# First rows of x sent ahead of the constants; odd layer's output weights further ahead in the order, no mix row in their staging buffers

## The chip, the cores and the metric

The kernel runs on one core of a Trainium2 chip. The metric is device time in microseconds (us), median of three runs; the kernel before takes 2293.11 us (2287.74 to 2295.61). Besides these there is one profiled execution, from which all rows below are taken.

## The reference, cut to what matters

Two layers over a sequence of 2048 rows of 1024 float32 values, each x <- x + RMSNorm(mixer(RMSNorm(x))). The even layer's mixer runs retention and stick-breaking attention side by side; the odd layer's runs a gated linear recurrence (HGRN2) and an RG-LRU. Both end the same way: the parts, each gated, are concatenated to eight blocks of 128 columns ("mix") and multiplied by an output matrix.

```python
def odd_mixer(h, w_in, w_out, lb, ...):
    proj = jnp.einsum('bsd,de->bse', h, w_in)
    hq, hf, hi, hg, lx, lg = split_cols(proj, ODD_SIZES)
    hc = rms_norm(hgrn2(hq, hf, hi, lb)).reshape(B, S, HG_VW) * jax.nn.silu(hg)
    hl = rg_lru(causal_conv(lx, ...), ...) * jax.nn.silu(lg)
    mix = jnp.concatenate([hc, hl], axis=-1)
    return jnp.einsum('bse,ed->bsd', mix, w_out)
...
for layer in range(DEPTH):
    h = rms_norm(x, pre_norm_w[layer])
    ...
    x = x + rms_norm(y, post_norm_w[layer])
```

## The kernel before, in words

The sequence is worked in two halves of 1024 rows, so there are four stages: even layer half 0, half 1, odd layer half 0, half 1. Each has a mixer phase (`stick` or `hgrn`) and then an output phase (`out_phase`). Products are float32 made of three fp32r products: each operand is split into a high part (cast on ACT) and a low part (difference on DVE), and each product of 128 contraction rows is three matmuls.

**Weights.** `load_w` (L118 to 133) loads 512 KB into a staging tile `raw` (pool `wr`, two buffers, one DMA on SP's queue, L127), casts it to `wh` on ACT (L131) and subtracts to `wl` on DVE (L132). The input projections (`proj`, L152) and the output weights go through the same two `raw` buffers, which are handed out in the order of the program.

**Mix.** A finished mix block of 128 columns by 512 rows is stored to DRAM (`mix_store`, L209, tensors `mixd`), except for the last of the eight, which is put straight into the operands `mh`, `ml` (`mix_direct`, L218 and L219). In the output phase `mix_rows` (L221 to 229) loads the other seven blocks for 128 rows back (L225, tile `mr`), casts on ACT (L227) and subtracts on DVE (L228). `mh`, `ml` lie in the tiles that held the transposed input `xh`, `xl` of the same 512 rows, so they can be written only once the last projection of these rows has run.

**Output phase.** Its output weights for the first 512 columns come as four pieces of 256 contraction rows (`W[0]`, L589, into pool `w2`); then `mix_rows` for rows 0 to 7 of 128 (pool `o2`, two buffers); then for each of the eight row groups 24 matmuls (L633) into one PSUM bank, named in turn `pp`, `z`, `o`. With `EARLY[layer]` = 1, row group 0 is fetched before that, from inside the last gate projection of the mixer phase, and staged in one of the two `raw` buffers (in `lru`, `lg_proj`, L762 to 764). `EARLY` is 0 for the even layer and 1 for the odd one.

**Order.** The program is written as one sequence; a scheduler gives each engine, and SP's DMA queue, its own fixed order, and each engine then works strictly in that order. `tc.high_priority(offset=n)` makes the scheduler treat the instructions inside as if they stood n instructions earlier. `tc.issue_after(d)` puts a DMA behind another on the queue. Pools are opened and closed like a stack: the pools of `out_phase` (`w2` 4 x (4 + 4) KB a partition, `o2` 2 x 3.5 KB, ...) begin at the place where those of `hgrn` began (`lru1` with `bd`, `lx`, `xc`, `r`, `ig` of 4 KB each; `lru5` with four tiles `ht` of 4 KB; `lrug` with `gt` of 2 KB; then `hg1`, `hg`, `hg4`). The last readers of these are in the last gate projection: `gt` times `ht` on DVE (L770), then `mix_direct` of `gt` (L218, L219).

**Start.** SP's queue begins with the identity matrix (L51) and two loads of `pre_norm_w` (L54), then the rows of x (L94). Each row of 128 is squared on ACT (L97), scaled on DVE (L99), transposed on PE (L112) and split (L114, L115). `stick` also builds a constant `past` in PSUM, with a copy on ACT (L378).

Of the kernel before, what the change touches and what calls it, by code (L numbers as in the profile page):

```python
# [21 lines left out]
KD = D // 128  # L22
EPS = 1e-6
LAG = 2
SHIFT = 1
EARLY = (0, 1)
LEVELS = (2, 4, 8, 16, 32, 64)


# [1 line left out]
def tile_trunk(ctx: ExitStack, tc: tile.TileContext, a: dict, out: bass.AP):  # L31
    nc = tc.nc
# [15 lines left out]
        return (o_bank[-1] if tag == "o" else ps_p).tile([128, 512], F32, tag=tag, name=tag)  # L48

    ident = const.tile([128, 128], F32, name="ident")  # L50
    nc.sync.dma_start(out=ident, in_=a["c_ident"])  # L51
    pre_w = const.tile([128, 2, KD], F32, name="pre_w")
    for i in range(2):
        nc.sync.dma_start(out=pre_w[:, i, :], in_=a["pre_norm_w"][i].rearrange("(k p) -> p k", p=128))  # L54
    mhalf = const.tile([128, 4], F32, name="mhalf")
    nc.vector.memset(mhalf, -0.5)
    state = const.tile([128, 512], F32, name="state")
# [16 lines left out]
    def scope(es, name, bufs, **kw):  # L74
        return es.enter_context(tc.tile_pool(name=name, bufs=bufs, reuse_waits="tile", **kw))

    def scope_o(es, bufs):
        o_bank.append(scope(es, "po", bufs, space=PSUM))
        es.callback(o_bank.pop)
        return o_bank[-1]  # L80
# [6 lines left out]
    def prep_rows(es, layer, half, ahead=2):  # L87
        p2, p8 = scope(es, "pr2", ahead), scope(es, "pr8", 8)
        rows = []

        def row(tt):
            i = half * 8 + tt
            xr = p2.tile([128, D], F32, tag="xr", name="xr")
            nc.sync.dma_start(out=xr, in_=x_in[i * 128:(i + 1) * 128, :] if layer == 0 else x1d[i])  # L94
            xn = p8.tile([128, D], F32, tag="xn", name="xn")
            ss = sm_p.tile([128, 1], F32, tag="ss", name="ss")
            nc.scalar.activation(out=xn, in_=xr, func=AF.Square, accum_out=ss)  # L97
            r = rstd_of(ss, 1, D)
            nc.vector.tensor_scalar(out=xn, in0=xr, scalar1=r, scalar2=None, op0=ALU.mult)  # L99
            rows.append(xn)  # L100
        return rows, row, p2

    def prep_cols(rows, layer):
        xh, xl = [], []

        def step(g, k):
            if k == 0:
                xh.append(xt_p.tile([128, KD, 512], F32R, tag="xh", name="xh"))
                xl.append(xt_p.tile([128, KD, 512], F32R, tag="xl", name="xl"))
            ps = bank("tr")  # L110
            for j in range(4):
                nc.tensor.transpose(ps[:, j * 128:(j + 1) * 128], rows[g * 4 + j][:, k * 128:(k + 1) * 128], ident)  # L112
            wk, hv = pre_w[:, layer, k:k + 1], xh[g][:, k, :]
            nc.scalar.activation(out=hv, in_=ps, func=AF.Copy, scale=wk)  # L114
            nc.vector.scalar_tensor_tensor(out=xl[g][:, k, :], in0=ps, scalar=wk, in1=hv.bitcast(F32), op0=ALU.mult, op1=ALU.subtract)  # L115
        return (xh, xl), step
# [20 lines left out]
    def proj_w(layer, col):  # L137
        ready[layer, col] = load_w(w_in[layer][:, col:col + 128], KD, 128)
# [82 lines left out]
    def mix_rows(half, M, tt, pool, tag):  # L221
        g, o = tt // 4, (tt % 4) * 128
        mh, ml = mix_slot(M, g)
        mr = pool.tile([128, 1024 if tag == "raw" else 896], F32, tag=tag, name="mr")[:, 0:896].rearrange("p (k t) -> p k t", k=7)
        d = nc.sync.dma_start(out=mr, in_=mixd[half][g][:, :, o:o + 128])  # L225
        hv = mh[:, 0:7, o:o + 128]
        nc.scalar.copy(out=hv, in_=mr)  # L227
        nc.vector.tensor_tensor(out=ml[:, 0:7, o:o + 128], in0=mr, in1=hv.bitcast(F32), op=ALU.subtract)  # L228
        return d.ins
# [57 lines left out]
    def ret_gate(half, heads, xT, t_p, g_p, M):  # L287
        for h in heads:
            def use(g, ps):
                if h == 3 and g == 1:  # L290
                    for tt in range(EARLY[0]):
                        mix_rows(half, M, tt, wr_p, "raw")
# [76 lines left out]
    def stick(half, xT, M):  # L369
        with ExitStack() as es:  # L370
            kv_p, qr_p, q_p, a_p, b_p, wt_p, g_p, t_p, r_p = (scope(es, n, b) for n, b in (
                ("skv", 8), ("sqr", 2), ("sq", 2), ("sa", 6), ("sb", 9), ("swt", 3), ("sg", 3), ("stmp", 2), ("srt", 1)))
            past = scope_o(es, 1).tile([128, 512], F32, tag="past", name="past")
            build = t_p.tile([128, 512], F32, tag="sg", name="build")
            nc.vector.memset(build, 0.0)
            nc.gpsimd.affine_select(out=build[:, 384:512], in_=build[:, 384:512], compare_op=ALU.is_gt, fill=1.0,
                                    base=0, pattern=[[-1, 128]], channel_multiplier=1)
            nc.scalar.copy(out=past, in_=build)  # L378
            D_ = [({}, {}, {}, {}) for _ in range(4)]

            def pair_proj(pr):
# [67 lines left out]
            def att(pr):  # L449
# [76 lines left out]
                for u in units + [None] * (2 if pr == 3 else 0):  # L526
                    bt = []
                    for i in range(4):
# [4 lines left out]
                        if u is not None and i == 3:  # L533
                            todo.extend((clock[0] + 1 + SHIFT + sj, back, gather, u, bt, sj) for sj in range(4))
                        if todo and todo[0][0] <= clock[0]:
                            _, fn, then, v, b, sj = todo.pop(0)
                            pend.append((then, v, sj) + fn(v, b, sj))
                            yield 437
                        if len(pend) > LAG:
                            then, *args = pend.pop(0)  # L540
# [29 lines left out]
    def out_phase(layer, half, M, following):  # L570
        prep_row = prep_step = xT = None
        with ExitStack() as es:
# [5 lines left out]
            else:  # L578
                x_p = scope(es, "ox", 8)
            early = EARLY[layer]  # L580
            mrs = [None] * early
# [3 lines left out]
            def piece(c, q, pool):  # L585
                return load_w(w_out[layer][:, c * 512:(c + 1) * 512], 2, 512, pool, order[2 * q:2 * q + 2])

            with tc.high_priority(offset=300):
                W = [[piece(0, q, w2_p) for q in range(4)], []]  # L589
            with tc.high_priority(offset=300):  # L590
                for tt in range(early, 8):
# [119 lines left out]
    def lru(half, xT, p1, p5, gt_p, sg_p, M):  # L711
# [50 lines left out]
        def lg_proj(j):  # L762
            def use_g(g, ps):
                if j == 3 and g == 1:
                    for tt in range(EARLY[1]):
                        mix_rows(half, M, tt, wr_p, "raw")
# [164 lines left out]
    with ExitStack() as es:  # L931
        rows, row, _ = prep_rows(es, 0, 0, 8)
        xT, step = prep_cols(rows, 0)
        for tt in range(8):
            row(tt)
            if tt in (3, 5):
                proj_w(0, 2048 if tt == 3 else 2560)
            if tt % 4 == 3:
                for k in range(KD):
                    step(tt // 4, k)  # L940
    for n, (layer, half) in enumerate(steps):
        M = {}
        if layer == 0:
            stick(half, xT, M)
            if half == 1:
                nc.vector.memset(state, 0.0)
                odd_const()
        else:
            with ExitStack() as es:
                hgrn(es, half, xT, M)  # L950
        xT = out_phase(layer, half, M, steps[n + 1] if n + 1 < len(steps) else None)
# [52 lines left out]
```

## Time and profile before

| | us |
|---|---|
| median of 3 runs | 2293.11 |
| lowest, highest | 2287.74, 2295.61 |
| the profiled execution, its own time | 2291.19 |
| its span, first to last instruction | 2289.3 |
| TensorE busy in it | 2210.1 |

A row of the timeline gives start, duration, engine, line, operation, output <- input, and the count merged into the row; in brackets the idle time of the engine before it and what ended that. A row of the windows gives for each stretch the busy time of each engine with the number of its instructions, the granted TensorE clock (1.00 is 2.4 GHz, 0.50 is 1.2 GHz), the share of DMA engines busy and GB/s.

### The profile page before, as it was taken

What the parts mean: (1) busy time and instruction counts of PE and PEld (TensorE: products, weight loads), DVE (VectorE), ACT (ScalarE), POOL (GpSimd) and SP (SyncE); (2) the same over time, 40 slices, a digit from 0 to 9 for tenths busy, and PEclk for the clock granted to TensorE, in tenths of its full rate; (3) what the DMA queues carried; (4) which work ended last, traced back from release to release, by engine and by line L of the source; (5) the groups of instructions that cost most, each with busy time, mean ns of one, the idle gap of its engine ahead of it and who ended that gap; (6) DMA issues with size and microseconds to landing.
All of it is one profiled execution on the core that took longest, in us unless ns stands there. A gap on an engine that the chain in (4) does not pass through costs nothing.

```text
span 2289.3 us, 31577 instructions
## 1 busy us (share of the span) xinstructions
PE 2210.1 (97%) x11392; PEld 1800.8 (79%) x11392; DVE 1391.7 (61%) x2049; ACT 1092.3 (48%) x2178; POOL 696.3 (30%) x988
## 2 busy tenths in 40 slices
PE   7999999999999999999899999999999999999998
PEld 6888787777878888787777887778877877878777
DVE  5554666674577776878888554555555535455543
ACT  5443545553466666767676433243245323433331
POOL 0422234411055454555663001222230013122400
PEclk9999999999999999999999999999999999999999
DMA  6433334346432232322313641111116511111161
GB/s 192 109 111 104 111 107 116 94 151 202 153 84 79 69 91 60 93 66 76 93 54 110 219 148 37 42 38 39 49 51 213 187 47 33 42 37 42 58 214 74
DMA packets 235804, 222.89 MB, mean 97 GB/s; under 512 B 21248, under 2 KB 181376, under 8 KB 235648
## 3 DMA queue, kind: packets, MB, share of 16 engines
q1 hardware_dynamic: 235488, 220.35, 31.2%
q8 instruction: 90, 1.47, 0.3%
q14 instruction: 66, 0.54, 0.1%
q0 software_dynamic: 160, 0.52, 0.1%
HBM read 147.43 MB, written 52.43 MB: 87 GB/s over the span
## 4 chain that ended last, share of the span: by engine, by line
PE 78%; DVE 9%; ACT 4%; DMA 3%; issue 3%; POOL 2%; SPq 0%; DVEq 0%; POOLq 0%; ACTq 0%
PE pp L152 42%; PE pp L633 5%; PE o L633 4%; PE o L514 4%; PE tr L499 4%; PE z L633 4%; DVE a L486 2%; PE z L473 2%; PE z L472 2%; PE z L887 2%; PE tr L112 1%; PE z L740 1%; DVE wtl L504 1%; DVE xc L734 1%; DVE wl L132 1%
## 5 line engine op out<-in xcount | busy, mean ns | idle before, releaser
L152 PE MATMUL pp<-xh,wh 128*128 128x512 f32 x1664 | 688.2, 414 | 6.9 <-DVE rst L356 6.2
L152 PE MATMUL pp<-xh,wl 128*128 128x512 f32 x1664 | 657.1, 395 | 0.0
L152 PE MATMUL pp<-xl,wh 128*128 128x512 f32 x1664 | 655.3, 394 | 0.0
L489 POOL TENSOR_TENSOR b<-b,a 128x511 f32<-128x511 f32 (+2 forms) x320 | 315.6, 987 | 181.9 <-DVE a L486 108.0
L152 PEld LDWEIGHTS pp<-xh,wl 128*128 128x128 f32 x1664 | 312.8, 188 | 68.2 <-issue 1.4
L152 PEld LDWEIGHTS pp<-xh,wh 128*128 128x128 f32 x1664 | 313.9, 189 | 60.4 <-issue 3.0
L152 PEld LDWEIGHTS pp<-xl,wh 128*128 128x128 f32 x1664 | 314.5, 189 | 48.6 <-issue 0.5
L486 DVE TENSOR_TENSOR_SCAN a<-a,past 128x512 f32<-128x512 f32 x192 | 244.4, 1275 | 74.7 <-ACT a L476 73.9
L476 ACT ACTIVATE a<-z 128x512 f32<-128x512 f32 (+2 forms) x320 | 172.2, 538 | 234.6 <-PE z L473 193.2
L132 DVE TENSOR_TENSOR wl<-raw,wh 128x1024 fp32r<-128x1024 f32 x136 | 170.2, 1257 | 129.8 <-ACT wh L131 129.5
L131 ACT CAST wh<-raw 128x1024 fp32r<-128x1024 f32 x136 | 142.8, 1053 | 187.9 <-PE pp L152 164.0
L71 POOL TENSOR_TENSOR rs<-rs,mhalf 128x1 f32<-128x1 f32 (+1 forms) x96 | 67.0, 698 | 515.6 <-DVE rs L70 502.8
L504 DVE TENSOR_TENSOR wtl<-tr,wth 128x512 fp32r<-128x512 f32 (+1 forms) x320 | 190.4, 596 | 44.4 <-ACT wth L503 43.4
L503 ACT CAST wth<-tr 128x512 fp32r<-128x512 f32 (+1 forms) x320 | 169.8, 531 | 69.4 <-PE tr L499 67.8
L499 PE MATMUL tr<-ident,b 128*128 128x128 f32 x1088 | 175.1, 275 | 10.6 <-DVE wtl L504 9.8
L499 PEld LDWEIGHTS tr<-ident,b 128*128 128x128 f32 x1088 | 133.1, 140 | 58.3 <-DVE wtl L504 17.1
L477 ACT ACTIVATE b<-z 128x512 f32<-128x512 f32 (+2 forms) x320 | 171.1, 535 | 0.1
L481 DVE TENSOR_TENSOR_SCAN a<-a,past 128x128 f32<-128x128 f32 (+3 forms) x128 | 104.5, 817 | 90.2 <-ACT a L476 89.3
L514 PE MATMUL o<-wth,v 128*128 128x512 f32 (+1 forms) x320 | 126.2, 394 | 1.1 <-ACT mol L520 1.1
L859 POOL TENSOR_TENSOR kg<-kg,t 128x256 f32<-128x256 f32 x96 | 71.3, 743 | 173.0 <-PE z L887 107.6
L479 POOL TENSOR_SCALAR_AFFINE_SELECT b<-b 128x128 f32<-128x128 f32 x128 | 42.3, 330 | 262.7 <-ACT b L477 246.7
L472 PE MATMUL z<-k,qh 128*128 128x512 f32 (+2 forms) x320 | 119.1, 372 | 1.9 <-DMA qh<-qrh 1.6
(216 smaller groups left out, 3592.5 us busy)
## 6 DMA issues: line engine op xcount, KB each, us to landing
raw<-in_even_w_in SPq DMA_DIRECT2D x56, 512.0 KB, 3.8
raw<-in_odd_w_in SPq DMA_DIRECT2D x48, 512.0 KB, 3.8
xr<-in_x SPq DMA_DIRECT2D x32, 512.0 KB, 4.3
xr<-x1d SPq DMA_DIRECT2D x32, 512.0 KB, 4.3
mr<-mixd SPq DMA_DIRECT2D x32, 448.0 KB, 4.8
qh<-qrh SPq DMA_DIRECT2D x64, 128.0 KB, 2.3
ql<-qrl SPq DMA_DIRECT2D x64, 128.0 KB, 2.4
x1d<-y SPq DMA_DIRECT2D x16, 512.0 KB, 2.9
```

The source lines that it names most:

```text
L132: nc.vector.tensor_tensor(out=wl, in0=raw, in1=wh.bitcast(F32), op=ALU.subtract)
L152: nc.tensor.matmul(ps, w[:, k, :], xx[g][:, k, :], start=(n == 0), stop=(n == 3 * KD - 1))
L472: nc.tensor.matmul(z[:, 0:n], qh[:, tcol], K[e, c][:, 0:n], start=True, stop=False)
L476: nc.scalar.activation(out=A[:, 0:n], in_=z[:, 0:n], func=AF.Sigmoid, scale=-0.125)
L477: nc.scalar.activation(out=B[:, 0:n], in_=z[:, 0:n], func=AF.Sigmoid, scale=0.125)
L486: nc.vector.tensor_tensor_scan(out=A[:, ::-1], data0=A[:, ::-1], data1=past[:, 0:1].to_broadcast([128, 512]), initial=carry[ti][:, 0:1], o ...
L489: nc.gpsimd.tensor_tensor(out=B[:, 0:n - 1], in0=B[:, 0:n - 1], in1=A[:, 1:n], op=ALU.mult)
L499: nc.tensor.transpose(tr[:, ti * 128:ti * 128 + 128], bt[ti][:, sj * 128:sj * 128 + 128], ident)
L503: nc.scalar.copy(out=wh[:, cols], in_=tr[:, cols])
L504: nc.vector.tensor_tensor(out=wl[:, cols], in0=tr[:, cols], in1=wh[:, cols].bitcast(F32), op=ALU.subtract)
L514: nc.tensor.matmul(O[:, cols], V[e, c][:, sj, :], w[:, cols], start=(diag and sj == 0 and w is wh), stop=(c == 0 and sj == 3 and w is wl))
L633: nc.tensor.matmul(ps, m[g][:, k, o:o + 128], w[:, k % 2, :], start=(n == 0), stop=(n == 3 * KD - 1))
```

## The change

`x`'s first two rows are queued ahead of the identity and `pre_norm_w`. The copy that makes `past` moves from ACT to DVE. For the odd layer the offset of the four first pieces of the output weights goes from 300 to 900, and row group 0 of mix is no longer fetched inside the last gate projection: all eight row groups now go through `o2`.

```diff
+AHEAD = (300, 900)
-EARLY = (0, 1)
+EARLY = (0, 0)
...
     ident = const.tile([128, 128], F32, name="ident")
-    nc.sync.dma_start(out=ident, in_=a["c_ident"])
     pre_w = const.tile([128, 2, KD], F32, name="pre_w")
-    for i in range(2):
-        nc.sync.dma_start(out=pre_w[:, i, :], in_=a["pre_norm_w"][i].rearrange("(k p) -> p k", p=128))
+
+    def load_const():
+        nc.sync.dma_start(out=ident, in_=a["c_ident"])
+        for i in range(2):
+            nc.sync.dma_start(out=pre_w[:, i, :], in_=a["pre_norm_w"][i].rearrange("(k p) -> p k", p=128))
...
-            nc.scalar.copy(out=past, in_=build)
+            nc.vector.tensor_copy(out=past, in_=build)
...
-            with tc.high_priority(offset=300):
+            with tc.high_priority(offset=AHEAD[layer]):
                 W = [[piece(0, q, w2_p) for q in range(4)], []]
...
         for tt in range(8):
             row(tt)
+            if tt == 1:
+                load_const()
```

## Rows read from the trace of the kernel before

**Rows 1.** The page: busy time of each engine.
```profile
PE 2210.1 (97%) x11392; PEld 1800.8 (79%) x11392; DVE 1391.7 (61%) x2049; ACT 1092.3 (48%) x2178; POOL 696.3 (30%) x988
```

**Rows 2.** Windows of 10 us: columns PE, PEld, DVE, ACT, POOL busy (instructions), clock, DMA.
```profile
490.00:500.00 10.00, 10.00 (x45) 8.26 (x45) 5.12 (x6) 4.11 (x5) 0.00 (x0) 1.00 0.85 252
...
1710.00:1720.00 10.00, 8.38 (x40) 6.61 (x38) 5.21 (x8) 3.58 (x6) 1.54 (x2) 1.00 0.24 79
1720.00:1730.00 10.00, 5.94 (x18) 4.14 (x19) 5.14 (x6) 3.74 (x5) 0.00 (x0) 0.86 0.68 209
1730.00:1740.00 10.00, 10.00 (x36) 7.62 (x36) 5.85 (x7) 5.05 (x8) 0.00 (x0) 0.80 0.50 151
...
2190.00:2200.00 10.00, 7.42 (x21) 4.81 (x22) 5.24 (x6) 3.49 (x4) 0.00 (x0) 0.83 0.78 242
```

**Rows 3.** Timeline of PE where odd half 0 passes into its output phase.
```profile
1717.97 0.39 PE L152 MATMUL pp<-xh,wl 128*128 128x512 f32 x1
1719.98 0.49 PE L633 MATMUL pp<-wh,mh 128*128 128x512 f32 x1 [1.62 <-ACT wh L131]
...
1738.92 0.39 PE L633 MATMUL o<-wh,mh 128*128 128x512 f32 x1
```

**Rows 4.** Timeline of PE at the same place of odd half 1.
```profile
2187.01 0.39 PE L152 MATMUL pp<-xh,wl 128*128 128x512 f32 x1
...
2200.64 0.39 PE L633 MATMUL z<-wh,mh 128*128 128x512 f32 x1
...
2206.08 0.39 PE L633 MATMUL o<-wh,mh 128*128 128x512 f32 x1
```

**Rows 5.** Timeline of SP's DMA queue around the first of these two places.
```profile
1701.58 0.55 SPq L225 DMA_DIRECT2D mr<-mixd  x1
1702.22 0.60 SPq L127 DMA_DIRECT2D raw<-in_odd_w_out  x1
...
1716.16 6.96 SPq L127 DMA_DIRECT2D raw<-in_odd_w_out  x3
1723.16 1.46 SPq L225 DMA_DIRECT2D mr<-mixd  x2
```

**Rows 6.** Timeline of ACT there, with the same cast in half 1 as last row.
```profile
1718.40 0.60 ACT L198 ACTIVATE sg<-pp 128x512 f32<-128x512 f32 x1 [3.21 <-PE pp L152]
1718.89 2.15 ACT L131 CAST wh<-raw 128x1024 fp32r<-128x1024 f32 x2
...
1729.91 0.94 ACT L227 CAST mh<-mr 128x896 fp32r<-128x896 f32 x1 [0.54 <-DMA mr<-mixd]
...
2198.59 0.94 ACT L227 CAST mh<-mr 128x896 fp32r<-128x896 f32 x1 [0.53 <-DMA mr<-mixd]
```

**Rows 7.** Timeline of DVE there.
```profile
1719.76 0.69 DVE L770 TENSOR_TENSOR gt<-gt,ht 128x512 f32<-128x512 f32 x1
1720.36 2.35 DVE L132 TENSOR_TENSOR wl<-raw,wh 128x1024 fp32r<-128x1024 f32 x2
1722.63 0.69 DVE L219 TENSOR_TENSOR ml<-gt,mh 128x512 fp32r<-128x512 f32 x1
...
1730.88 1.09 DVE L228 TENSOR_TENSOR ml<-mr,mh 128x896 fp32r<-128x896 f32 x1 [0.25 <-ACT mh L227]
```

**Rows 8.** DMA issues of the page: KB each, median us from issue to landing.
```profile
mr<-mixd SPq DMA_DIRECT2D x32, 448.0 KB, 4.8
raw<-in_odd_w_out SPq DMA_DIRECT2D x16, 512.0 KB, 5.0
```

**Rows 9.** The start, timeline: SP's queue and ACT.
```profile
0.81 0.40 SPq L51 DMA_DIRECT2D ident<-in_c_ident  x1
...
2.35 2.00 SPq L94 DMA_DIRECT2D xr<-in_x  x4
...
10.32 0.58 ACT L378 COPY past<-build 128x512 f32<-128x512 f32 x1
```

**Rows 10.** The start, a window of 1 us (columns as in the windows above).
```profile
3.00:4.00 1.00, 0.00 (x0) 0.00 (x0) 0.00 (x0) 0.00 (x0) 0.00 (x0) 1.00 0.50 4
```

## The prediction

> **What bounds the kernel now.** I read the page first: TensorE is busy 2210.1 of 2289.3 us [rows 1], so an edit can win only where PE waits, and loses wherever it makes PE wait longer. The windows come next, to find those places. Inside the even layer's first passage into its output phase PE has no gap (10.00 of 10 us) [rows 2]; at the odd layer's it is busy 8.38 and 5.94 us of two stretches of 10, and the clock is granted at 0.86 and 0.80, and the second half of the odd layer shows the same, 7.42 and 0.83 [rows 2]. So the change works at the two places where the kernel loses time, besides the start, and the rest was read from timelines of these places, engine by engine.
>
> In odd half 0 the last projection matmul starts at 1717.97 and the output phase starts at 1719.98, held by the weight cast; the third row group (bank `o`) begins at 1738.92 [rows 3]. Without a gap it would begin two row groups after 1718.2. A row group is 2206.08 - 2200.64 = 5.44 us [rows 4], so 1718.2 + 10.88 = 1729.1: the passage loses 9.8 us. In half 1 the same reckoning is 2187.24 + 10.88 = 2198.1 against 2206.08, 8.0 us [rows 4]. Both together, 17.8 us, are all that the odd edits can win.
>
> **What sets this order.** Piece 0 of the output weights is issued at 1702.22 [rows 5] and lands some 5.0 us later [rows 8], but is cast at 1718.89, though ACT stood idle 3.21 us before 1718.40 [rows 6]. What it follows is DVE's last reading of `ht` and `gt` (L770, 1719.76, in the order just ahead of `wl`, 1720.36) [rows 7]. The places fit: `w2` takes the first 32 KB of what `hgrn` used, where `lru1` ends at 20 KB and the four `ht` of `lru5` follow to 36 KB; `o2` takes 32 to 39 KB, where the last `ht` and `lrug`'s `gt` lie. Mix rows agree: row group 0, staged in `raw`, is issued at 1701.58, but row group 1, from the same `mixd` columns, only at 1723.16 [rows 5], after the last reader of `gt` has started at 1722.63 [rows 7]. I read this as: nothing of `w2` is put in the order before the last use of `ht`, nothing of `o2` before the last use of `gt`, whatever offset stands on it. An offset of 300 already reaches far enough: at 40 + 8 + 6 + 2 instructions per 10 us [rows 2] it is some 50 us.
>
> **The change part by part.**
>
> *Offset 900 for the odd layer's pieces.* The two `raw` buffers are handed out in program order, so a larger offset can't pass the projections' weights. With the mix row out of them, pieces 0 and 1 both load during the last projections, not piece 1 at 1716.16 [rows 5]. But their casts still stand behind L770, and piece 1 was there almost in time already: the two casts follow each other without a break that the row shows, 2.15 us for both [rows 6]. Gain: a few tenths of a us at most. Pieces 2 and 3 still wait for the `raw` buffers, freed by the two `wl` that end at 1722.71 [rows 7]. I take 0.
>
> *No mix row in `raw`.* This takes away a DMA, a cast and a subtraction in each half, all beside PE's work, so nothing is won there. What is lost is the one row group that stood ready. Row group 0 now takes the place that row group 1 has now: first load of `o2`, issued at 1723.16 behind the weight pieces [rows 5], cast at 1729.91 when it lands, done at 1730.85 [rows 6], its low part at 1731.97 [rows 7]. All 24 matmuls of the row group need it, so PE, which now works from 1719.98 on between two waits, stands still until 1730.85. Then two row groups, 10.88 us, and what the clock takes: it is granted at 0.86 and 0.80 in two stretches of 10 us, thus at its lower level for 2.8 + 4.0 us in half 0, and for 3.4 us in half 1 (0.83) [rows 2]; half the work of such time is lost, 3.4 and 1.7 us. After a pause of 12 us I expect it again and take 2.4 us, the ends being 0.8 (half of the lower figure, part of the time falling into the pause) and 3.4. Bank `o` begins at 1730.85 + 10.88 + 2.4 = 1744.1, against 1738.92: **+5.2 us** (+3.6 to +6.2). In half 1 the cast stands at 2198.59 [rows 6], so 2199.53 + 10.88 + 2.4 = 2212.8 against 2206.08 [rows 4]: **+6.7 us** (+5.1 to +7.7). From there the row groups follow without a wait: a load of 4.8 us [rows 8] with a cast of 0.94 and a subtraction of 1.09 [rows 6, 7], two in flight, gives a row group each 3.4 us, and 5.44 are needed. `post_norm_w`, the second half's weights and the next rows of x are queued behind these mix loads and shift with them by about what PE shifts.
>
> *First two rows of x ahead of the constants.* x was issued at 2.35, and can go at 0.81 [rows 9]: 1.54 us sooner for two rows; the other six stay behind the same three constants. ACT squares row after row there, and the copy of `past`, 0.58 us at 10.32 [rows 9], stood between two rows. It goes to DVE, idle in that window [rows 10]. At most 1.54 + 0.58 = 2.1 us. At least 0, if rows 2 and 3, whose place in the queue does not change, set the first transposed block. I take 1.2, a little over the middle, because the copy on ACT goes in any case. `past` of half 1 moves in the same way at a place where PE has other work; if that cover were gone it would cost 0.6 us.
>
> The loads of `pre_norm_w` keep the DMA engines 0.50 busy for 4 GB/s [rows 10]; they now run among the rows of x. The Trainium skill (DMA: Bandwidth & Descriptors, "Rules for kernel authors") says that many small transfers are mostly overhead and should be coalesced; by it, half of the two microseconds would be taken from x again and the gain would be 0.2 instead of 1.2. The trace shows the share, not yet the collision.
>
> **The sum.** 5.2 + 6.7 - 1.2 = +10.7 us, with ends 3.6 + 5.1 - 2.1 = +6.6 and 6.2 + 7.7 - 0 = +13.9. The profiled execution took 2291.19 us, so 2301.9; it lies 1.9 us under the median of 2293.11, on which the same sum gives **2303.8 us**, +0.47%.
>
> **The rivals.**
>
> *The stall goes (faster).* The order of `w2` and `o2` may not be tied to `ht` and `gt`, and the offset may be what held piece 0. Then all four pieces and row group 0 are cast before the last projection ends, and PE runs through, as it does in the even layer, where no mix row is staged early either [rows 2]. That wins 9.8 + 8.0 + 1.2 = 19.0 us: 2274.1. The point from which it decides: row group 0 must be issued by about 1718.4 - 4.8 - 0.94 - 1.09 = 1711.6; break-even for half 0 is a cast that ends by 1738.92 - 10.88 - 2.4 = 1725.6. Against it: the idle ACT beside a landed piece, and row group 1 issued 21.6 us after row group 0 [rows 5, 6].
>
> *Row group 0 passes pieces 2 and 3 in the queue (no change).* If it is issued at 1720.4, when `ht` is read, it lands 4.8 us later [rows 8], at 1725.2, and PE starts at 1726.2; pieces 2 and 3 come one load later and hold k-blocks 4 to 7. Bank `o` begins at 1726.2 + 10.88 + 2.4 = 1739.5, +0.6 in half 0, and as far behind its last projection in half 1, 2187.24 + 21.3 = 2208.5, +2.4; with the start +1.8, so 2294.9. For it: 448 KB need no buffer of `raw`. Against it: the pieces now have the larger offset, and stand ahead of the mix rows already [rows 5].
>
> *The offset does nothing at all*: that is part of my forecast, and its price is 0.
>
> **How the numbers follow.** Chances: 0.64 for the forecast, 0.18 for the faster rival, 0.18 for the one without change. A measurement of this kernel tells 0.3%, 6.9 us, from no change, so the borders are 2286.2 and 2300.0. Of the forecast 0.04 lies under 2300, of the third case nearly all is within: faster 0.18, same 0.22, slower 0.60. The range leaves out the faster rival and takes in the other two: from 2289 (the third case with the runs' own spread) to 2309 (+13.9 and 2 us of spread).
>
> **What would show it.** In the profile after, at the odd passage: pieces 0 and 1 issued well before the last projection ends, yet cast behind L198 and L770; the first `mr` load behind two weight loads; PE's first output matmul waiting some 12 us, released by L227 or L228 and not by L131; the windows there with a lower clock than now. The start should show the first output of L152 one to two microseconds sooner. The forecast is wrong if casts of output weights stand ahead of L770, if an `mr` load stands ahead of pieces 2 and 3, or if PE's wait there is under 7 us.

## The result and the profile after

The changed kernel takes 2307.16 us (median of 5, 2302.90 to 2314.16) against 2293.11 us of the kernel before, a ratio of 1.0071 with a 95% interval of 1.0055 to 1.0087: slower by 0.7%. The profiled execution took 2302.90 us with a span of 2301.0 us, against 2291.19 and 2289.3 before, so the profiled pair differs by 11.7 us, and the medians by 14. The forecast was +10.7 us, 2303.8.

TensorE does the same work, 2209.6 us of it. The line numbers of the changed kernel are four higher at these places (L637 was L633, L231 was L227, L774 was L770). The first lines of the list of PE's waits after are these (line waited for: us in total, times, longest us):

```profile
PE pp L637 <- ACT mh L231: 24.3, 2, 12.4
PE tr L503 <- DVE wtl L508: 9.7, 26, 0.9
```

The two waits at the head are new. Both stand where the odd layer enters its output phase, one in each half, and both end with the cast of a mix row (L231, `mh`), not with the cast of a weight piece as before [rows 3]. The timeline of PE after shows them from both sides (start us, us, what ended the idle time before it in brackets), half 0 first:

```profile
1717.60 0.39 PE L156 MATMUL pp<-xh,wl 128*128 128x512 f32 x1
1729.97 0.79 PE L637 MATMUL pp<-wh,mh 128*128 128x512 f32 x1 [11.98 <-ACT mh L231]
...
1743.25 0.39 PE L637 MATMUL o<-wh,mh 128*128 128x512 f32 x1
...
2190.65 0.39 PE L156 MATMUL pp<-xh,wl 128*128 128x512 f32 x1
2203.39 0.79 PE L637 MATMUL pp<-wh,mh 128*128 128x512 f32 x1 [12.35 <-ACT mh L231]
...
2217.15 0.39 PE L637 MATMUL o<-wh,mh 128*128 128x512 f32 x1
```

Call the time from the start of the last projection matmul to the first matmul of bank `o` the **passage**. Before it was 20.95 us in half 0 [rows 3] and 19.07 in half 1 [rows 4]; after it is 25.65 and 26.50. The difference, 4.70 + 7.43 = 12.1 us, is all that the profiled pair shows of the loss.

Who is late is told by SP's queue and by ACT after, the places of [rows 5] and [rows 6]:

```profile
1721.23 1.52 SPq L131 DMA_DIRECT2D raw<-in_odd_w_out  x2
1722.86 1.35 SPq L229 DMA_DIRECT2D mr<-mixd  x2
```

```profile
1718.52 1.98 ACT L135 CAST wh<-raw 128x1024 fp32r<-128x1024 f32 x2
1720.40 0.62 ACT L222 CAST mh<-gt 128x512 fp32r<-128x512 f32 x1
1724.85 1.04 ACT L135 CAST wh<-raw 128x1024 fp32r<-128x1024 f32 x1 [3.83 <-DMA raw<-in_odd_w_out]
1727.42 1.04 ACT L135 CAST wh<-raw 128x1024 fp32r<-128x1024 f32 x1 [1.53 <-DMA raw<-in_odd_w_out]
1728.98 0.94 ACT L231 CAST mh<-mr 128x896 fp32r<-128x896 f32 x1 [0.51 <-DMA mr<-mixd]
```

Row group 0 is loaded at 1722.86 behind weight pieces 2 and 3 and cast at 1728.98; PE starts 12.4 us after its last projection matmul. Why SP came to pieces 2 and 3 only at 1721.23 stands in its own waits after, stretch 1700 to 1732:

```profile
SPq L131 <- DVE wl L136: 15.4, 2, 14.7
```

It stood 14.7 us in front of one weight load, until a `raw` buffer came free. Everything behind it in the queue stood too. That line turned out to be the heart of the case. The queue stood there in the kernel before as well, longest for the subtraction of the staged row:

```profile
SPq L127 <- DVE ml L228: 9.3, 1, 9.3
```

But there row group 0 had gone ahead of it, at 1701.58 [rows 5].

Windows after (us, busy time and instructions of PE, PEld, DVE, ACT, POOL, granted clock, DMA share, GB/s), against [rows 2]:

```profile
1720.00:1730.00 10.00, 0.03 (x1) 0.04 (x1) 5.45 (x7) 4.04 (x5) 0.00 (x0) 0.54 0.73 233
1730.00:1740.00 10.00, 10.00 (x34) 7.74 (x35) 4.25 (x5) 3.41 (x5) 0.00 (x0) 0.77 0.52 154
```

PE is all but empty for a whole window, and the clock lies at its lower level into the next one (0.77, which is 4.6 us at half speed): the first ten output matmuls start some 0.43 us or more apart, the later ones 0.23.

### The profile page after: what moved, and what is told of

The parts are those of the page before. It is cut to its first block, busy times and chain, and to the rows that moved or that the text cites. A ratio compares the mean times of both kernels' runs of the same rounds, so it can differ in the third digit from the quotient of the medians.

```text
span 2301.0 us, 31577 instructions
## 1 busy us (share of the span) xinstructions
PE 2209.6 (96%) x11392; PEld 1803.7 (78%) x11392; DVE 1394.3 (61%) x2051; ACT 1091.4 (47%) x2176; POOL 696.4 (30%) x988
## 4 chain that ended last, share of the span: by engine, by line
PE 78%; DVE 9%; ACT 4%; DMA 4%; issue 3%; POOL 2%; SPq 0%; DVEq 0%; POOLq 0%; ACTq 0%
PE pp L156 42%; PE pp L637 5%; PE o L518 4%; PE o L637 4%; PE tr L503 4%; PE z L637 4%; DVE a L490 2%; PE z L477 2%; PE z L476 2%; PE z L891 2%; DMA mr<-mixd 1%; PE tr L116 1%; PE z L744 1%; DVE wtl L508 1%; DMA xr<-in_x 1%
```

## The experiments

Ratios are to the kernel before on the same chip.

**e1, the missing row alone**, in the kernel before:

```
-EARLY = (0, 1)
+EARLY = (0, 0)
```

> The kernel before with one edit: row group 0 is no longer staged in a raw buffer (EARLY of the odd layer 1 to 0); offset and start stay as before. My theory, that this one edit makes the whole loss: PE's first output matmul of the odd layer waits some 12 us in each half, released by the cast of mh, the two passages to bank o are longer than before by 4 to 5 and by 6.7 to 7.5 us, and the time is longer by 11 to 12.5 us, a ratio of 1.0050 to 1.0056. Rival, that the row only costs together with the offset of 900, which puts the weight pieces ahead of the mix rows: row group 0 then comes back ahead of pieces 2 and 3, and the ratio is under 1.002. Rival for the part of the loss that the profile of the changed kernel did not show (its median is 14 us over that of the kernel before, its profiled pair 11.7 apart): if that part belongs to this edit, the ratio is 1.0065 or more.

Measured: ratio 1.0071 (1.0053 to 1.0089), median 2306.70, span of the profile 2301.1. Passages 26.83 and 25.25, that is 5.9 and 6.2 us longer than in the profile of the kernel before, where I had written 4 to 5 and 6.7 to 7.5. PE's first wait in the list:

```profile
PE pp L633 <- ACT mh L227: 24.1, 2, 12.4
```

The same two waits, without the offset and without the early rows of x: this one edit makes a loss as large as that of the whole change. The ratio lies over the 1.0050 to 1.0056 of my theory and over the 1.0065 of the last rival, so the part of the loss that the profiled pair did not show seems to belong to this edit too; the interval reaches down to 1.0053, so this run alone doesn't decide that (e5 shows where the part is).

**e2, everything but the missing row**, the changed kernel with `EARLY = (0, 1)`:

> The changed kernel with row group 0 staged in a raw buffer again (EARLY of the odd layer back to 1); the offset of 900, the early rows of x and the copy of past on DVE stay. My theory: the passages are those of the kernel before, and only the start gain is left, 0.4 (as the profiled pair showed) to 1.2 us (as forecast), a ratio of 0.9995 to 0.9998, which the interval can't tell from 1. Rival, that the start edits cost something later which hides the gain: a ratio over 1.001, with one of the even layer's stages longer than before by over 2 us.

Measured: 0.9998 (0.9987 to 1.0008). Passages 18.77 and 19.00. So offset, early rows and the moved copy together change nothing that can be measured; the rival with a hidden cost has no room left over 0.08%.

**e3, the changed kernel again**:

> The changed kernel itself, once more, beside the others of this call. Nothing is left out or added. If the 2.4 us between its first ratio (1.0071) and the difference of the profiled pair (11.7 us, 0.51%) came from the runs' spread, this ratio lies at 1.0045 to 1.0065 and its interval holds 1.0055. If something that the first profile did not catch costs it 4 us more, the ratio is again 1.007 or more, and the profile shows where.

Measured: 1.0059 (1.0045 to 1.0073), median 2305.64. Passages 25.54 and 25.65. It lies 0.12% under the first ratio; the two intervals share 1.0055 to 1.0073, so the difference can be the runs' spread.

**e5, the offset alone**, in the kernel before:

```
+AHEAD = (300, 900)
-            with tc.high_priority(offset=300):
+            with tc.high_priority(offset=AHEAD[layer]):
                 W = [[piece(0, q, w2_p) for q in range(4)], []]
```

> The kernel before with one edit: the odd layer's weight pieces carry the offset of 900 instead of 300. The compiled order of instructions is that of the kernel before on all five engines, so this run also shows what one and the same program does from execution to execution. My theory: ratio 1.000, its interval within 0.998 to 1.002. For the point still open on the size of the loss: the passage from the last projection matmul to bank o took 20.95 us in odd half 0 of the profiled kernel before, yet 18.8 to 19.1 in its half 1 and in both halves of the kernel that keeps the row. If 20.95 was a chance of that execution, this profile shows 18.7 to 19.3 in half 0, and the reference that the forecast took for half 0 was some 2 us too late; if it belongs to the program, it shows 20.5 to 21.5 again.

Measured: 1.0003 (0.9991 to 1.0015). Passages 19.34 and 19.23, where the profile of one and the same program had shown 20.95 and 19.07. PE's timeline, to be read against [rows 3]:

```profile
1719.86 0.39 PE L153 MATMUL pp<-xh,wl 128*128 128x512 f32 x1
1721.86 0.49 PE L634 MATMUL pp<-wh,mh 128*128 128x512 f32 x1 [1.62 <-ACT wh L132]
1723.52 0.80 PE L634 MATMUL pp<-wl,mh 128*128 128x512 f32 x1 [1.16 <-DVE wl L133]
...
1739.20 0.39 PE L634 MATMUL o<-wh,mh 128*128 128x512 f32 x1
```

So 20.95 was a chance of the one execution on which the forecast rested. That is most of the missing part of the loss (11.7 us in the profiled pair, 14 in the medians): the changed kernel's profile was compared with a half 0 that was 2 us worse than usual.

**e4, other memory under the weights and the mix rows.** The kernel is the changed one. `ht` of j = 3 goes to a pool of its own behind a filler (`hole`, of which one column is set, on GpSimd). By the places that the prediction reckoned, `w2` then lies over the three `ht` that are read earlier. The two buffers `o2` become two pools of one buffer, the first of them over the filler. The tile `junk` shares the buffers of `hs`. The edit, cut:

```
-            w2_p, p2, p1, y_p = scope(es, "w2", 4), scope(es, "o2", 2), scope(es, "o1", 1), scope(es, "y", 8)
+            w2_p, p2 = scope(es, "w2", 4), (scope(es, "o2", 1), scope(es, "o2b", 1))
...
-                    mrs.append(mix_rows(half, M, tt, p2, "mr"))
+                    mrs.append(mix_rows(half, M, tt, p2[tt % 2 if layer == 0 or tt == 0 else (tt + 1) % 2], "mr"))
...
-                    ht = p5.tile([128, 1024], F32, tag="ht", name="ht")
+                    ht = p5[j == 3].tile([128, 1024], F32, tag="ht", name="ht")
...
-        lp1, lp5, lpg = scope(es, "lru1", 1), scope(es, "lru5", 4), scope(es, "lrug", 1)
+        lp1, lp5a = scope(es, "lru1", 1), scope(es, "lru5", 3)
+        hole = scope(es, "hole", 1).tile([128, 888], F32, name="hole")
+        nc.gpsimd.memset(hole[:, 0:1], 0.0)
+        lp5b, lpg = scope(es, "lru5b", 1), scope(es, "lrug", 1)
...
```

> The changed kernel with another placing in on-chip memory and the same arithmetic: the odd layer's tiles are laid out so that the output weights w2 and one of the two staging buffers of mix rows lie over memory whose last reader comes early, instead of over ht and gt. This takes away what I hold to be the cause of the wait. My theory: all four pieces and row group 0 are loaded and cast ahead of the last projection's end, PE passes from the last projection to the output matmuls with a gap under 2 us in both halves, the clock keeps its higher level there, and against the kernel before 9.8 and 8.0 us are won, with the start 0.4 more: 2293 - 18 = 2275, a ratio of 0.992 (the time that the prediction gave to its faster rival). If row group 1 comes late, up to 5.4 us a half are given back: ratio 0.992 to 0.997. Rival, that the order hangs on the offset, on SP's queue or on the mix stores and not on memory: the casts stay behind the last silu, the wait stays at 12 us a half, ratio 1.005 to 1.007.

Measured: **0.9942** (0.9928 to 0.9955), median 2279.80: faster than both kernels. Passages 11.24 and 11.11, two row groups and nothing else. ACT's timeline shows the casts of the four weight pieces and of row group 0, which the changed kernel has behind its last silu (L202), ahead of it (the last silu of e4 starts at 1724.99):

```profile
1709.18 2.01 ACT L135 CAST wh<-raw 128x1024 fp32r<-128x1024 f32 x2
...
1716.17 1.05 ACT L135 CAST wh<-raw 128x1024 fp32r<-128x1024 f32 x1 [0.15 <-DMA raw<-in_odd_w_out]
1717.12 0.94 ACT L231 CAST mh<-mr 128x896 fp32r<-128x896 f32 x1
1718.02 1.05 ACT L135 CAST wh<-raw 128x1024 fp32r<-128x1024 f32 x1
```

and PE passes through without a gap:

```profile
1722.47 0.39 PE L156 MATMUL pp<-xh,wl 128*128 128x512 f32 x1
1722.70 0.39 PE L638 MATMUL pp<-wh,mh 128*128 128x512 f32 x1
...
1733.71 0.50 PE L638 MATMUL o<-wh,mh 128*128 128x512 f32 x1
```

The arithmetic is the same; the pools, and with them the addresses, differ. So the place of these casts in the order hangs on how the pools lie in memory. Whether e4 needs the offset of 900 was not tried. Of the 18 us that I had written down, 13 came: the 9.8 of half 0 was reckoned from the same 20.95 us; from 19.0 it is 7.9, and 7.9 + 7.9 = 15.8 us, or 0.9931, lies inside the interval.

**e9, the weights alone apart**: e4 with one pool of two buffers `o2` again. By the same reckoning its first buffer lies over the filler and its second over the last `ht`:

```
-            w2_p, p2 = scope(es, "w2", 4), (scope(es, "o2", 1), scope(es, "o2b", 1))
+            w2_p, p2 = scope(es, "w2", 4), scope(es, "o2", 2)
...
```

> The kernel with the placing of e4_memory_apart, but only the weights w2 lie over memory that is free early; both staging buffers o2 of the mix rows again lie, as one pool, partly over the last ht and over gt. This parts the two halves of the gain of e4. My theory: each tile's place in the order hangs on the last reader of the memory under its own pool. So all four weight pieces are cast ahead of the last projection's silu and free the raw buffers, the queue is not blocked and row group 0 is loaded early, but its cast still stands behind the last cast of gt on ACT; PE waits about 4 us a half (3 to 4.5) for that cast, then 0.5 for the low part, and two row groups follow, 10.9, with up to 2.4 for the clock: passages of 15.0 to 18.0 us, against 11.1 to 11.2 with both apart and 18.8 to 21 in the kernel before; ratio to the kernel before 0.9955 to 0.9985. Rival 1, that the weights were all of it: passages under 13, ratio 0.994 or less. Rival 2, that weights early are worth nothing while row group 0 is late: passages over 18.5, ratio over 0.999.

Measured: 0.9979 (0.9968 to 0.9990). Passages 17.77 and 17.29. ACT's timeline:

```profile
1712.38 1.05 ACT L135 CAST wh<-raw 128x1024 fp32r<-128x1024 f32 x1 [0.58 <-DMA raw<-in_odd_w_out]
...
1719.08 0.62 ACT L222 CAST mh<-gt 128x512 fp32r<-128x512 f32 x1 [1.49 <-DVE gt L775]
1719.60 0.93 ACT L231 CAST mh<-mr 128x896 fp32r<-128x896 f32 x1
```

The last piece is cast 6 us before the mix row, which still stands right behind the last cast of `gt`. Its load was issued at 1708.15, so nothing but its place in the order holds this cast. PE waits 3.63 us for it. The load of row group 1, into the second buffer, does wait for the memory under it; SP's queue, stretch 1708 to 1720:

```profile
SPq L229 <- DVE gt L775: 10.4, 1, 10.4
```

It goes at 1719.07, when L775 has read the last `ht`. Pool by pool, then: the casts into `w2` and from `o2` move each with its own pool, and each costs PE something of its own. That the order goes by the last reader of anything under the whole pool, while a load waits for its own buffer alone, fits both runs; how the scheduler decides it is not shown.

**e6, row group 0 ahead of pieces 2 and 3 in the queue**, memory as in the changed kernel:

```
-W = [[piece(0, q, w2_p) for q in range(4)], []]
+W = [[piece(0, q, w2_p) for q in range(2 if layer else 4)], []]
 ...
     mrs.append(mix_rows(half, M, tt, p2, "mr"))
+    if layer and tt == 0:
+        with tc.issue_after(mrs[0]):
+            W[0] += [piece(0, q, w2_p) for q in (2, 3)]
```

> The changed kernel with the odd layer's queue in another order: the load of row group 0 is issued ahead of pieces 2 and 3 instead of behind them, and is cast ahead of them on ACT. The order over memory is left as it is. My theory, that PE's wait ends with row group 0's place in the queue: the load goes at about 1721.9 instead of 1722.9, lands 4.3 us later and is cast at once, since ACT need not cast pieces 2 and 3 first; PE starts at 1727.2 instead of 1729.97 where the last projection is as early as in the changed kernel, a wait of 9 to 10 us instead of 12, the passages are 2 to 3 us shorter each, ratio to the kernel before 1.0030 to 1.0045. Rival, that DMA time is what the wait is made of (six loads at once share it): row group 0 lands no sooner, or pieces 2 and 3 hold PE at the fifth block of k by as much; passages within 0.7 us of those of the changed kernel (25.3 to 26.8), ratio 1.0055 to 1.0070.

Measured: 1.0002 (0.9990 to 1.0014), passages 19.26 and 19.21. The whole loss is gone, more than twice what I expected. SP's queue and then ACT show what I had wrong:

```profile
1705.99 0.55 SPq L229 DMA_DIRECT2D mr<-mixd  x1
...
1720.62 1.52 SPq L131 DMA_DIRECT2D raw<-in_odd_w_out  x2
1722.35 1.53 SPq L229 DMA_DIRECT2D mr<-mixd  x2
```

```profile
1717.90 1.98 ACT L135 CAST wh<-raw 128x1024 fp32r<-128x1024 f32 x2
1719.78 0.62 ACT L222 CAST mh<-gt 128x512 fp32r<-128x512 f32 x1
1720.31 0.94 ACT L231 CAST mh<-mr 128x896 fp32r<-128x896 f32 x1
```

I expected the load at 1721.9. It went at 1705.99, 13 us before `ht` and `gt` were last read, and waited for neither: its buffer was free all along, though the prediction's map puts the last `ht` under it. In the changed kernel nothing held that load but the weight pieces in front of it, which waited 14.7 us for a `raw` buffer. What still stands late is only the cast (1720.31 on ACT, right behind the cast of `gt`), and PE waits 3.92 us for it instead of 12.

**e7 and e10, the pause filled**: the changed kernel with matmuls put ahead of the odd layer's row groups on PE:

```
+if layer == 1:
+    tr = bank("tr")
+    fw = W[0][0][0]
+    for n in range(30):      # 46 in e10
+        nc.tensor.matmul(tr, fw[:, 0, 0:128], fw[:, 1, :], start=(n == 0), stop=(n == 29))
```

> The changed kernel with 30 matmuls more in each odd half, on PE alone, into a bank that nobody reads: they use piece 0's cast weights, so they run from about 1720.6, when that cast ends, into the wait for row group 0. This measures the clock's part of the loss by itself. My theory: the pause costs PE's lower clock level behind it (first output matmuls 0.43 us apart instead of 0.23, 2.2 to 2.7 us in each half); with the pause cut to under 4 us at its head, the fillers take any low stretch themselves, the row groups begin at the same time but run at the higher level, passages of 23.0 to 24.0 us instead of 25.3 to 26.8, ratio to the kernel before 1.0035 to 1.0045. Rival, that the level falls whatever PE does there: the row groups behind still start 0.43 us apart, and passages stay at 25.3 or more, longer by up to 4 us if the fillers themselves run at the lower level to their end; ratio 1.0055 to 1.0085.

> The kernel of e7_pause_filled with 46 filling matmuls instead of 30 in each odd half. With 30 the fillers ran from 2.0 to 9.1 us behind the last projection matmul, 0.237 us apart, a pause of 4.2 us followed, and the row groups behind it still lost 2.4 us to the lower clock level. 46 end where row group 0 is ready (11.3 us of the wait of 13.3, or some tenths later). My theory, that the pause right ahead of the row groups, even one of 4 us, is what brings the lower level: now the row groups start 0.23 us apart and two of them take 10.9 to 11.5 us instead of 13.2 (from the first output matmul to bank o), ratio to the kernel before 1.0040 to 1.0050. Rival, that the level follows from something else at this place (the pause of 1.6 to 2 us ahead of the fillers, or the loads and casts): two row groups again take 12.8 us or more, ratio 1.0055 to 1.0075.

Measured: e7 1.0062 (1.0048 to 1.0076), passages 26.53 and 26.80; e10 1.0043 (1.0031 to 1.0056), passages 25.48 and 24.58. The interval of e10 overlaps those of the changed kernel, so the answer is read from the traces. PE in e7, then in e10:

```profile
1724.21 0.39 PE L156 MATMUL pp<-xh,wl 128*128 128x512 f32 x1
1726.22 7.10 PE L603 MATMUL tr<-wh 128*128 128x512 f32 x30 [1.62 <-ACT wh L135]
1737.50 0.50 PE L642 MATMUL pp<-wh,mh 128*128 128x512 f32 x1 [4.18 <-ACT mh L231]
```

```profile
1719.93 10.72 PE L603 MATMUL tr<-wh 128*128 128x512 f32 x46 [1.62 <-ACT wh L135]
1731.72 0.50 PE L642 MATMUL pp<-wh,mh 128*128 128x512 f32 x1 [1.07 <-ACT mh L231]
...
1743.40 0.39 PE L642 MATMUL o<-wh,mh 128*128 128x512 f32 x1
```

Their windows, two of e7 and two of e10:

```profile
1730.00:1740.00 10.00, 5.42 (x20) 3.88 (x19) 4.64 (x4) 3.98 (x4) 0.00 (x0) 0.92 0.75 234
1740.00:1750.00 10.00, 10.00 (x41) 8.11 (x40) 3.62 (x4) 3.51 (x5) 0.00 (x0) 0.90 0.68 199
```

```profile
1720.00:1730.00 10.00, 10.00 (x44) 8.30 (x45) 4.49 (x5) 3.11 (x4) 0.00 (x0) 1.00 0.64 196
1730.00:1740.00 10.00, 8.54 (x36) 6.41 (x36) 4.51 (x5) 4.14 (x6) 0.00 (x0) 1.00 0.48 146
```

With 30 fillers, my theory failed: the fillers ran at the higher level, but after them came 4.18 us without work (4.28 in half 1), and from the first output matmul to bank `o` it took 13.24 us in half 0 and 13.42 in half 1, no less than in the three profiles of the missing row without fillers (12.7 to 14.1, mean 13.4). With 46 the clock is granted at 1.00 throughout, and the same stretch takes 11.68 and 11.69 us, a little over the 10.9 to 11.5 that I had written but far from the rival's 12.8. So the pause right ahead of the row groups is what costs the clock here, and one of 4 us did it as well as one of 12; its price is 13.4 - 11.7 = 1.7 us a half. The forecast's 2.4 us stood against two row groups without any wait, 10.88 us, and 13.4 - 10.88 = 2.5 agrees with it; of the 0.8 us between the two prices, 0.39 is a wait for the low part (L232) that the slower matmuls cover.

**e8, four rows of x ahead of the constants**, in the kernel of e2:

```
-            if tt == 1:
+            if tt == 3:
                 load_const()
```

> The kernel that keeps the row (EARLY of the odd layer 1), with four rows of x ahead of the constants instead of two. This asks why the start gained nothing: in the profiles the first projection matmul starts at 15.0 us in the kernel before and in the changed kernel alike. My theory, that rows 2 and 3 set the first transposed block and still stand behind the constants: with all four ahead, the third transposed row starts 1 to 1.6 us sooner than 12.27, and the first projection matmul at 13.5 to 14.2, unless the first weight block, cast at 12.77, is next in line (then 14.2 to 14.7). Rival, that the small constant loads take from x whatever they are given, as in the rule cited with the prediction: the third transposed row within 0.3 us of 12.27 and the first projection matmul at 14.7 to 15.3.

Measured in the profile (ratio 0.9991, 0.9978 to 1.0005, which can't tell): the third transposed row at 10.92, the fourth at 12.39, the first projection matmul at 14.75, a little over the 14.2 to 14.7 that I had written. It is held by ACT, which casts the first weight block (from 13.07 on) ahead of the first `xh`. The changed kernel's start, PE:

```profile
7.85 0.69 PE L116 MATMUL tr<-ident,xn 128*128 128x128 f32 x2 [7.85 <-DVE xn L103]
9.04 0.69 PE L116 MATMUL tr<-ident,xn 128*128 128x128 f32 x2 [0.50 <-DVE xn L103]
12.27 0.69 PE L116 MATMUL tr<-ident,xn 128*128 128x128 f32 x2 [2.53 <-DVE rs L74]
...
14.99 0.80 PE L156 MATMUL pp<-xh,wh 128*128 128x512 f32 x1 [0.56 <-ACT xh L118]
```

In the kernel before, the same four rows of the timeline begin at 9.34, 10.82, 12.29 and 15.01. The two rows sent ahead do come 1.5 and 1.8 us sooner; the third, still behind the constants, does not, and the first block needs four. Sending four wins 1.35 us there and loses most of it to the weight block, next in line: 0.24 us are left.

## Why the prediction was right and wrong

The steps that failed are two terms of the sum and one reading. The term for the missing row in half 0 was +5.2 us and measures +7.0, because bank `o` at 1738.92 [rows 3], from which it was taken, was 2 us later than usual; the term for the start was -1.2 and measures 0.0; and row group 0's late load was put down to `gt`, where the runs show a queue blocked by weight pieces. The place of the loss and the wait in it were right.

**What bounds the kernel, and where the change acts**: right. The loss lies in the two passages, PE waits some 12 us in each (11.98 and 12.35), released by the cast of `mh` (L231), with the weight casts still behind the last silu (L202) and the windows at 0.54 and 0.77. Each of these was named ahead.

**Offset of 900, taken at 0**: right. In e5's trace PE and SP's queue work in the order of the kernel before, and it measured 1.0003.

**Missing row, half 1, +6.7**: right. The rows-kept profiles (before, e2, e5, e8) give passages of 19.07, 19.00, 19.23 and 18.87 in half 1, those with the row missing (after, e1, e3) 26.50, 25.25 and 25.65, mean 25.8: +6.8.

**Missing row, half 0, +5.2**: mis-sized, and not in what it forecast but in what it was taken from. The forecast passage was 20.95 + 5.2 = 26.15; measured are 25.65, 26.83 and 25.54, mean 26.0. The reference of 20.95 [rows 3] was the chance: 18.77, 19.34 and 18.89 in e2, e5 and e8, mean 19.0. So the term is +7.0. The rows held a warning: one code, run twice, at 20.95 and 19.07 [rows 3, 4].

**Start, -1.2**: wrong. It is 0.0 (15.01 to 14.99 at the first projection matmul). The prediction named the case, that rows 2 and 3 set the first block, as its lower end and then took the middle. The copy of `past` hid in the same wait: row 3 is squared on ACT at 10.87 after and at 10.84 before. Nor do the rows cited show DVE idle at the copy's place: [rows 10] is the stretch 3 to 4 us, and the copy stood at 10.32. The Trainium skill's rule that small transfers are mostly overhead (DMA: Bandwidth & Descriptors, "Rules for kernel authors") says nothing of what they take from other loads; the gain of 0.2 was the prediction's own estimate from it. That number was nearer, but not for its reason: the two rows came 1.5 and 1.8 us sooner with the small loads right behind them.

With the two terms mended the sum is 7.0 + 6.8 - 0.0 = +13.8 us, 1.0060, against measured 1.0071 (1.0055 to 1.0087) and 1.0059 (1.0045 to 1.0073); on the median of 2293.11 it is 2306.9 against 2307.16. This is a sum of measured terms, not a forecast.

**What sets the order**: right for the casts, wrong for the load. That the casts into `w2` and from `o2` go with the memory under their pools is borne out by e4 and e9. But they don't wait for its last reader: the casts of pieces 0 and 1 start at 1718.89 [rows 6], ahead of L770 at 1719.76 [rows 7] that the prediction had them follow, and in the changed kernel at 1718.52, ahead of L774 at 1719.38. It is the order on ACT, behind the last silu, that holds them; read by start times, casts of output weights stood ahead of L770 in the kernel before already, so this sign of being wrong could not tell anything. And the prediction read row group 1's late load [rows 5] as held by `gt` as well; e6 issued row group 0's load 13 us ahead of the last readers of `gt`. In the changed kernel the queue in front of the load was blocked by weight pieces that waited for `raw`, and the time only coincided with the last reading of `gt`.

**The rivals.** The faster one fell for this change, since the offset moves nothing; its time of 2274.1 was reached to within 6 us by e4, by another way. The third case, row group 0 ahead of pieces 2 and 3, did not happen either, but e6 made it happen, and it gave 2291.23 where 2294.9 stood: PE then starts 4.3 us after its last projection matmul, not 8.2, because the load went at 1705.99 and not at the 1720.4 of the forecast.

**Not settled** is what made the passage of 20.95 us in the one execution. Its timeline has a wait of 2.14 us for a weight cast (ACT L131, at 1726.57) and, by the granted clock [rows 2], 6.8 us of the lower level. In e5, half 0 has the 6.8 us (a window at 0.66) without the wait, at 19.34, and half 1 a like wait (1.96) with 3.4 us of the lower level, at 19.23. Why both fell together once is open.

## What to carry to other kernels

A load that waits for its buffer at the head of an in-order queue delays every load behind it, so before a staged tile is given up, ask what will stand in front of its new load and what that waits for: here 14.7 us of a blocked queue cost 6.9 us of TensorE time twice, and a swap of two places (e6) gave them back. Where casts of the next phase are late though their data are there, look at whose memory their tiles take over; laying them over memory whose last reader comes earlier won 0.58% against the kernel before, though ACT's casts show no wait for memory, only a late place in the order. And take the reference of a forecast from each place where the same code runs: a difference of 2 us between two halves was a measure of the error.

## What the hardware showed beside that

**The clock's level falls at other places in each execution of one program.** The window of 360 to 370 us of the kernel before and of e5, whose instructions come in the same order:

```profile
360.00:370.00 10.00, 8.18 (x42) 6.64 (x41) 4.55 (x9) 2.42 (x8) 3.37 (x6) 1.00 0.33 78
```

```profile
360.00:370.00 10.00, 8.18 (x33) 6.42 (x32) 4.31 (x9) 1.99 (x7) 3.37 (x6) 0.83 0.24 54
```

Both have PE at 8.18 us; one has the higher level throughout, the other 0.83 and nine matmuls fewer. Ahead of the odd layer's first output phase the profiles show from one to five such stretches, and the last projection matmul of half 0 moves with their number: 1716.57 to 1717.97 with one (before, e6, e9, e10), 1717.60 and 1718.40 with two (after, e1), 1719.58 to 1720.51 with three (e2, e3, e5), 1722.47 with four (e4), 1724.21 and 1724.43 with five (e7, e8). The mean places of those with five and with one give (1724.3 - 1717.4) / 4 = 1.7 us for each, an estimate, since these are not all one program. This is more than the start was forecast to win (1.2 us), so one profile can't tell an edit of that size.

**A short pause costs about as much clock as a long one.** Behind 12 us without work two row groups took 13.4 us (the mean of six), behind 4.18 and 4.28 us (e7) 13.2 and 13.4, and behind 1.07 and 0.16 us (e10) 11.7.
